# Group norm and gate of RWKV in four steps, laid beside the scan in another rhythm, and the first output columns ahead of the last units

## The chip, the cores and the metric

The kernel runs on one core of a Trainium2 chip. The metric is the device time of one execution in microseconds (us). The kernel before took 2945.2 us (median of three runs, 2944.56 to 2947.44).

## The reference, cut to what matters

One layer of an encoder over 1024 positions and 1024 channels, all in float32. Between two feed-forward halves stands a mixer. Its RWKV branch ends, for the sum y of a forward and a backward scan with 8 heads of 64 channels, in a group norm, a bonus and a gate, and both branches then go through projections:

```
y = moveaxis(ys[:, 0] + flip(ys[:, 1], axis=0), 0, 1)
y = (y - mean) * rsqrt(var + GN_EPS)  * ln_w + ln_b        # mean, var per head
y = y + sum over dirs of sum(r * k_dir * r_k, per head) * v
y = (y * (sigmoid(gd) @ g2)) @ w_o
merged = sigmoid(g_hy) * y_hy + sigmoid(g_rw) * y_rw
x = x + merged @ w_out
```

## The kernel before, in words

Every dense product is three matmuls (`mm3`): operands are split into a high part (ScalarE) and a remainder (VectorE or GpSimd), and hi\*lo, lo\*hi and hi\*hi are summed in PSUM. A dense group of 128 output channels and 512 positions with 512 inputs is twelve matmuls of 128x512 (4 times 3), with 1024 inputs 24.

The sequence is cut into 8 blocks of 128 positions. `Rwkv.run` walks through them in about ten steps a block (it yields after each): products with the inverted matrix, the next block's scores and its triangular inversion on VectorE (`eliminate`: `rw_lt`, fourteen pairs of small `rw_el`/`rw_x` operations, `rw_xt`; L955 to L980), two halves of the scan (`psS`, `psY`), and four steps that finish the inverse. The backward scan's results are stored in DRAM at the mirrored block, so blocks b and 7-b are complete together.

The first 64 steps of the scan run beside the gates' columns (`mixer_gates`). The last 25 run beside two other generators: `hyena_out` (16 dense groups, PSUM tile `pz`) and units of norm and gate (`RwkvPost.unit(b, u)`): one unit takes the block pair (b, 7-b) and half of the channels, 128x512 numbers. It loads y of both directions, k_dir of both, r, v and the gate's operands (ten DMAs), multiplies by a block of ones (`rp_ones`: head sums, L1466, L1468), squares, forms the inverse deviation (`head_rstd_steps`: `rp_head`, VectorE's `hr_` chain, `ident`), multiplies by the gate (`rp_gd`, `rp_g2`, L1491) and stores to `d_yo`. Each unit's tiles have one buffer in that phase. Five units (pairs 3, 3, 2, 2, 1) run there in 25 steps, one per step of the scan. The other three, (1,1), (0,0), (0,1), run in `mixer_out` in lockstep after the scan, and then come the 16 dense groups of `rw_out` (`mo_ps`), in two halves of positions: the first half needs only blocks 2 to 5, the second the others. Each group's result is merged with `sg` and `mh` (four DMAs of 128 KB per group, L1528) and split. Then the PSUM pool is closed, and 16 groups of 24 matmuls with `w_out` follow (`wo_ps`, another pool of three banks).

PE matmuls issued through `InOrder` keep the order in which they were written. All else is ordered by the framework's scheduler at build time, one fixed queue per engine; all DMAs stand on SyncE's queue (SP). `w_st` and `z_st` share two buffers.

Of the kernel before, what the change touches and what calls it, by code (L numbers as in the profile page):

```python
# [773 lines left out]
def head_rstd_steps(nc, te, ve, pool, rb, psum, sq, head, ident, scale, lo, eps):  # L774


    n = sq.shape[1] // P
    ps = psum.tile([P, 512], F32, name="psA", tag="psA")
    for t in range(n):
        te.matmul(ps[:, 2 * t : 2 * t + 2], sq[:, ts(t, P)], head, start=True, stop=True)  # L780
# [24 lines left out]
    return out
# [370 lines left out]
def mixer_in(tc, I, ident, wp, hl, scl, h2, h2ctx, dr):  # L1176
# [3 lines left out]
    with ExitStack() as ctx:  # L1180
# [69 lines left out]
        def rwkv_tile(j, width, u, o):  # L1250
# [152 lines left out]
def split_half(nc, wp, pool, src):  # L1403

    hi, lo = [pool.tile([P, 4, 512], F32R, name=n, tag=n) for n in ("s_hi", "s_lo")]
    for h in range(2):
        st = wp.tile([P, 2, 512], F32, name="z_st", tag="w_st")
        for j in range(2):
            x = src(2 * h + j)
            nc.sync.dma_start(st[:, j] if len(x.shape) == 2 else st[:, j].rearrange("p (b t) -> p b t", t=P), x)  # L1410
        split_from(nc, hi[:, 2 * h : 2 * h + 2], lo[:, 2 * h : 2 * h + 2], st, "act", "dve")
    return hi, lo
# [6 lines left out]
class RwkvPost:  # L1419
# [15 lines left out]
    def bank(self):  # L1435
        return self.psum.tile([P, 512], F32, name="psA", tag="psA")

    def unit(self, b, u):

        nc, te, dr, I = self.nc, self.te, self.dr, self.I  # L1440
        ve = nc.vector
        sl = slice(b, 8 - b, 7 - 2 * b)
        flat = lambda x: x.rearrange("p b q t -> p (b q t)")
        g = {}
        for n, m, d in (("y0", "y", 0), ("y1", "y", 1), ("k0", "kd", 0), ("k1", "kd", 1), ("r", "r", 0), ("v", "v", 0)):
            g[n] = self.work.tile([P, 2, 2, P], F32, name="rp_" + n)
            nc.sync.dma_start(g[n], dr[m][d][:, sl, 2 * u : 2 * u + 2])
        gd, g2 = [], []
        for n, r in ((0, slice(0, P)), (1, slice(P, P + 32))):
            rows = r.stop - r.start  # L1450
            gd.append(self.work.tile([P, 2, P], F32, name=f"rp_gd{n}")[0:rows])
            nc.sync.dma_start(gd[n], dr["gd"][r].rearrange("p (b t) -> p b t", t=P)[:, sl])
            g2.append(self.work.tile([P, 2, P], F32, name=f"rp_g2{n}")[0:rows])
            nc.sync.dma_start(g2[n], I["rw_g2"][r, ts(u, 256)].rearrange("p (q c) -> p q c", c=P))
        yield
# [18 lines left out]
        norm = head_rstd_steps(nc, te, ve, self.work, lambda: g["k1"].rearrange("p b q (e f) -> p (b q) e f", e=2), self.psum,
                               sq, self.head, self.ident, 1.0 / 64.0, None, GN_EPS)
# [7 lines left out]
        ve.tensor_tensor(flat(y), flat(y), pb, ALU.mult)  # L1483
# [3 lines left out]
        yield  # L1487
        ps = self.psum.tile([P, 2, 2, P], F32, name="psA", tag="psA")
        for q in range(2):
            for n in range(2):  # L1490
                te.matmul(ps[:, :, q], g2[n][:, q], gd[n], start=n == 0, stop=n == 1)  # L1491
# [5 lines left out]
def mixer_out(tc, I, ident, wp, dr, yp, early, begin, done, half_done):  # L1497
# [3 lines left out]
    with ExitStack() as ctx:  # L1501
        pool = lambda name, bufs, **k: ctx.enter_context(tc.tile_pool(name=name, bufs=bufs, **k))
        one = pool("mo1", 1)
        m_hi = one.tile([P, KD, L], F32R, name="m_hi")
        m_lo = one.tile([P, KD, L], F32R, name="m_lo")
        with ExitStack() as c2:
            pool2 = lambda name, bufs, **k: c2.enter_context(tc.tile_pool(name=name, bufs=bufs, **k))
            yb, two = pool2("mo2", 1), pool2("mo3", 2)
            pm, pq = pool2("mop", 3, space=PSUM), pool2("mopq", 4, space=PSUM)
            halves = lambda t: lambda q: dr["yo"][:, 4 * t : 4 * t + 4, q]  # L1510
# [6 lines left out]
            blocks = lambda a, j: a[ts(j, P)].rearrange("p (b t) -> p b t", t=P)  # L1517
            for t in range(2):
                if t:
                    y.append(split_half(nc, wp, yb, halves(1)))  # L1520
                for j in range(KD):
                    w = col_weights(nc, wp, I["rw_out"][:, ts(j, P)], 4, lo_eng="dve")
                    sg, mh = [two.tile([P, 512], F32, name=n) for n in ("mo_sg", "mo_mh")]
                    for x, n in ((sg, "sg"), (mh, "mh")):
                        x4 = x.rearrange("p (b t) -> p b t", t=P)
                        for h in range(2):
                            b = ORDER[4 * t + 2 * h]
                            nc.sync.dma_start(x4[:, ts(h, 2)], blocks(dr[n], j)[:, b : b + 2])  # L1528
# [23 lines left out]
def hybrid_layer_kernel(ctx: ExitStack, tc: tile.TileContext, I: dict, out: bass.AP):  # L1552
# [60 lines left out]
    with ExitStack() as c2:  # L1613
# [3 lines left out]
        with ExitStack() as c3:  # L1617
# [5 lines left out]
            def units():  # L1623
                todo = [post.unit(b, u) for b, u in ((3, 0), (3, 1), (2, 0), (2, 1), (1, 0))]
                next(todo[0])
                for g, n in zip(todo, todo[1:] + [None]):
                    for i in range(5):
                        if next(g, None) is None and i == 4 and n:
                            next(n)
                        yield  # L1630

            bg = units()
# [4 lines left out]
            for g in (bg, hy):  # L1637
                for _ in g:
                    pass
    with ExitStack() as ctx2:  # L1640
# [17 lines left out]
        mixer_out(tc, I, ident, wp, dr, zp, early, begin, lambda d, t: live["nm"].add(live["xT"][:, d, ts(t, 512)], t), normed)  # L1658
# [49 lines left out]
```

## Time and profile before

| | us |
|---|---|
| median of three runs | 2945.2 |
| the profiled execution | 2941.74 |
| its span | 2939.9 |
| PE busy | 2733.1 (93%) |
| DVE busy | 1233.9 (42%) |
| ACT busy | 905.4 (31%) |

PE is TensorE's matmuls, DVE VectorE, ACT ScalarE, POOL GpSimd, SP SyncE's DMA queue. Times of day ("at 1990") are us from the span's start. A square bracket in a timeline row is the engine's idle time before the row and what ended it.

### The profile page before, as it was taken

Reading aid. Unit: us, or ns where it says so; the run is one execution under the profiler, and the core shown is the slowest. Engines: PE = TensorE matmul, PEld = TensorE weight load, DVE = VectorE, ACT = ScalarE, POOL = GpSimd, SP = SyncE. Lnnn points to the kernel's source line nnn. Section 1 sums busy time; section 2 is a strip of 40 time slices with the busy share of each in tenths; the row PEclk is TensorE's granted clock in tenths of the full one; section 3 lists DMA queues with packets and bytes.
Section 4 is the critical chain, followed back from the end, with each engine's and each line's share of the span. In section 5 each row is a group of like instructions: output and inputs, shape, how many; then the busy total and the mean of one; then the engine's idle time right before and its main releaser. Section 6 shows DMA issues by size and latency. Waiting matters only on the chain. (4 is left out here: it accounts for less than half of the span.)

```text
span 2939.9 us, 46164 instructions
## 1 busy us (share of the span) xinstructions
PE 2733.1 (93%) x19440; PEld 2207.4 (75%) x19440; DVE 1233.9 (42%) x2142; ACT 905.4 (31%) x1515; POOL 549.9 (19%) x351
## 2 busy tenths in 40 slices
PE   7999999999788899996899998897899999999998
PEld 6888888888566677774777777675678888888887
DVE  4111010110556769798565567655560101111014
ACT  4111111111355543334454454421332111111112
POOL 2323233232422200000000000000023332323322
PEclk8999999999899999998999999897999999999999
DMA  4111111111432345545435335446731111111112
GB/s 122 51 43 54 40 58 43 40 57 44 154 82 76 111 148 170 166 125 161 114 101 157 101 104 153 150 126 199 224 101 43 51 53 40 58 43 52 46 29 90
DMA packets 414494, 277.66 MB, mean 94 GB/s; under 512 B 53571, under 2 KB 377359, under 8 KB 413648
## 3 DMA queue, kind: packets, MB, share of 16 engines
q1 hardware_dynamic: 414288, 274.72, 31.7%
q8 instruction: 153, 2.51, 0.4%
q14 instruction: 53, 0.43, 0.0%
HBM read 203.75 MB, written 70.91 MB: 93 GB/s over the span
## 5 line engine op out<-in xcount | busy, mean ns | idle before, releaser
L43 PE MATMUL pgu<-hThi,w_hi 128*128 128x512 f32 x1408 | 554.0, 393 | 0.9 <-issue 0.8
L45 PE MATMUL pgu<-hThi,w_lo 128*128 128x512 f32 x1408 | 551.4, 392 | 0.0
L44 PE MATMUL pgu<-hTlo,w_hi 128*128 128x512 f32 x1408 | 547.3, 389 | 0.5 <-DVE hTlo L37 0.3
L210 DVE TENSOR_TENSOR silu<-silu,pgu 128x512 f32<-128x512 f32 x88 | 60.5, 688 | 892.2 <-PE pgu L45 882.8
L33 ACT CAST w_hi<-w_st 128x1024 fp32r<-128x1024 f32 (+1 forms) x180 | 175.1, 974 | 531.2 <-PE pgu L44 320.4
L37 POOL TENSOR_TENSOR w_lo<-w_st,w_hi 128x1024 fp32r<-128x1024 f32 x100 | 240.4, 2404 | 419.2 <-ACT w_hi L33 419.1
L45 PEld LDWEIGHTS pgu<-hThi,w_lo 128*128 128x128 f32 x1408 | 264.3, 188 | 60.7
L44 PEld LDWEIGHTS pgu<-hTlo,w_hi 128*128 128x128 f32 x1408 | 264.3, 188 | 59.5 <-DVE hTlo L37 0.7
L43 PEld LDWEIGHTS pgu<-hThi,w_hi 128*128 128x128 f32 x1408 | 264.6, 188 | 55.0 <-issue 1.2
L43 PE MATMUL pdn<-g_hi,wd_hi 128*128 128x512 f32 x704 | 275.6, 391 | 3.1 <-DVE xT L227 3.1
L44 PE MATMUL pdn<-g_lo,wd_hi 128*128 128x512 f32 x704 | 275.1, 391 | 2.0 <-POOL g_lo L37 2.0
L45 PE MATMUL pdn<-g_hi,wd_lo 128*128 128x512 f32 x704 | 275.4, 391 | 1.5 <-POOL wd_lo L37 1.5
L227 DVE SCALAR_TENSOR_TENSOR xT<-pdn,xT 128x512 f32<-128x512 f32 x192 | 132.4, 690 | 315.3 <-PE pdn L45 315.3
L43 PE MATMUL pw<-hThi,w_hi 128*128 128x512 f32 (+1 forms) x448 | 185.2, 413 | 17.6 <-DVE nm_h L123 10.0
L45 PE MATMUL pw<-hThi,w_lo 128*128 128x512 f32 (+1 forms) x448 | 185.1, 415 | 12.1 <-DVE w_lo L1224 12.1
L37 POOL TENSOR_TENSOR wd_lo<-wdst,wd_hi 128x512 fp32r<-128x512 f32 (+1 forms) x112 | 133.0, 1189 | 332.7 <-ACT wd_hi L33 330.0
L37 POOL TENSOR_TENSOR g_lo<-silu,g_hi 128x512 fp32r<-128x512 f32 x88 | 113.9, 1294 | 397.2 <-ACT g_hi L33 397.2
L44 PE MATMUL pw<-hTlo,w_hi 128*128 128x512 f32 (+1 forms) x448 | 183.4, 409 | 0.0
L33 ACT CAST wd_hi<-wdst 128x512 fp32r<-128x512 f32 (+1 forms) x112 | 64.4, 576 | 378.7 <-PE pdn L44 361.6
L37 POOL TENSOR_TENSOR hTlo<-nm_h,hThi 128x512 fp32r<-128x512 f32 x16 | 23.1, 1445 | 841.7 <-ACT hThi L33 841.7
L43 PEld LDWEIGHTS pdn<-g_hi,wd_hi 128*128 128x128 f32 x704 | 132.5, 188 | 31.9 <-ACT wd_hi L33 4.2
L44 PEld LDWEIGHTS pdn<-g_lo,wd_hi 128*128 128x128 f32 x704 | 132.6, 188 | 30.7 <-POOL g_lo L37 2.9
(312 smaller groups left out, 4259.2 us busy)
## 6 DMA issues: line engine op xcount, KB each, us to landing
w_st<-in_ffn_w_gu SPq DMA_DIRECT2D x88, 512.0 KB, 3.8
w_st<-in_w_in SPq DMA_DIRECT2D x59, 512.0 KB, 4.3
wdst<-in_ffn_w_down SPq DMA_DIRECT2D x64, 256.0 KB, 2.8
wdst<-in_ffn_w_down SPq DMA_DIRECT2D x48, 192.0 KB, 2.4
d_kf<-kout SPq DMA_DIRECT2D x32, 256.0 KB, 3.6
hy_k<-d_kf SPq DMA_DIRECT2D x32, 256.0 KB, 3.2
w_st<-in_w_out SPq DMA_DIRECT2D x16, 512.0 KB, 5.3
d_X<-sh_x SPq DMA_DIRECT2D x12, 512.0 KB, 3.5
```

The lines of the kernel that those rows point to most:

```text
L33: nc.scalar.copy(hi, src)
L37: eng.tensor_tensor(lo, src, hi.bitcast(F32), ALU.subtract)
L43: te.matmul(out, lhs[0], rhs[0], start=first, stop=False)
L44: te.matmul(out, lhs[0], rhs[1], start=False, stop=False)
L45: te.matmul(out, lhs[1], rhs[0], start=False, stop=last)
L210: nc.vector.tensor_tensor(sl, sl, pu, ALU.mult)
L227: nc.vector.scalar_tensor_tensor(xa, ps, 0.5, xa, ALU.mult, ALU.add)
```

## The change

A unit has four steps instead of five: its loads are a function of their own (`load`, k and r ahead of y), the gate's product stands in the last step, the sum of both y behind the k operations. In the 25 scan steps a table decides: units skip the steps i % 10 = 3 and 4 (scores with inversion, first half of the scan), so 5 units and the first step of the sixth run there; dense groups of `hyena_out` fall on i % 10 = 0, 2, 3, 4, 6, 8, and on the first four of the last five. `mixer_out` takes up the sixth unit, loads both units of pair 0 in one set of ten DMAs twice as wide, and has the first weights, gates and the first half of `y` (`y0`) issued before. Gate and merge loads cover two groups each (256 KB DMAs), and `w_out`'s groups use the same four PSUM banks (`mo_ps`) as `rw_out`'s. The mixer's own projections compute the same numbers. The core of the diff:

```
+    def load(self, b, n):
...
+        for k, m, d in (("k0", "kd", 0), ("k1", "kd", 1), ("r", "r", 0), ("y0", "y", 0), ("y1", "y", 1), ("v", "v", 0)):
+            nc.sync.dma_start(g[k], dr[m][d][:, sl, 2 * u0 : 2 * u0 + n])
...
@@ unit @@
-        ve.tensor_tensor(flat(y), flat(y), flat(g["y1"]), ALU.add)
         for i in range(2):
             ve.tensor_tensor(k[:, i], k[:, i], g["k1"][:, 1 - i, :, ::-1], ALU.add)
         for q in range(2):
             ve.scalar_tensor_tensor(k[:, :, q], g["r"][:, :, q], vec(q, 2), k[:, :, q], ALU.mult, ALU.mult)
+        ve.tensor_tensor(flat(y), flat(y), flat(g["y1"]), ALU.add)
         yield
...
@@ mixer_out @@
-            pm, pq = pool2("mop", 3, space=PSUM), pool2("mopq", 4, space=PSUM)
-            y = [split_half(nc, wp, yp, halves(0))]
-            post = RwkvPost(nc, nc.tensor, I, dr, ident, pool2("mo4", 1), pool2("mo5", 3), pq)
-            units = [post.unit(b, u) for b, u in ((1, 1), (0, 0), (0, 1))]
-            for _ in range(6):
-                for g in units:
-                    next(g, None)
+            pq = pool2("mopq", 3, space=PSUM)
+            w = [weights(0), weights(1)]
...
+            gates(0, 0)
+            g = post.load(0, 4)
+            units = [rest, post.unit(0, 0, g(0)), post.unit(0, 1, g(1))]
+            while units:
+                units = [u for u in units if next(u, u) is not u]
...
-        pm = pool("mop2", 3, space=PSUM)
...
@@ beside the scan @@
             for i, _ in enumerate(rw):
-                next(bg, None)
-                if (i + 1) * 16 // 25 > i * 16 // 25:
-                    next(hy, None)
+                last = i >= 20
+                if last or i % 10 not in (3, 4):
+                    next(unit)
+                    at += 1
+                    if at % 4 == 0:
+                        b, u = todo[at // 4]
+                        unit = post.unit(b, u, post.load(b, (u, 2))(u))
+                if i % 10 in ((0, 1, 2, 3) if last else (0, 2, 3, 4, 6, 8)):
+                    next(hy)
...
+            y0 = split_half(nc, wp, zp, lambda st, h: nc.sync.dma_start(st, dr["yo"][:, 0:4, 2 * h : 2 * h + 2]))
```

On PE, behind the last matmuls of the dense groups `pz` and of the scan (`psY`), stood before the three units' sums (`rp_ones`) and squares (`rp_head`):

```order
L55 MATMUL pz<-s_hi,w_lo 128x512
L1466 MATMUL psA<-rp_y_17657,rp_ones 128x512
L1468 MATMUL psA<-rp_k_17661,rp_ones 128x512
L1466 MATMUL psA<-rp_y_17677,rp_ones 128x512
L1468 MATMUL psA<-rp_k_17681,rp_ones 128x512
L1466 MATMUL psA<-rp_y_17697,rp_ones 128x512
L1468 MATMUL psA<-rp_k_17701,rp_ones 128x512
L780 MATMUL psA<-rp_head,rp_y_17659 128x2 x4
```

and stands now:

```order
L55 MATMUL psY<-rw_t_16287,rw_s 64x64 x8
L55 MATMUL psA<-rp_y_17541,rp_ones 128x512
L55 MATMUL psA<-rp_k_17543,rp_ones 128x512
L43 MATMUL mo_ps<-s_hi,w_hi 128x512
L44 MATMUL mo_ps<-s_lo,w_hi 128x512
L45 MATMUL mo_ps<-s_hi,w_lo 128x512
L43 MATMUL mo_ps<-s_hi,w_hi 128x512
L55 MATMUL psA<-rp_head,rp_y_17542 128x2 x4
```

One unit's sums stand there, then the dense groups begin: 36 matmuls of `mo_ps` stand ahead of the sums of pair 0, 16 more ahead of its first `ident`, 5 ahead of the last, and 135 behind them.

On DVE, the end of the first inversion in this phase (`rw_x` last pair to `rw_xt`) had a unit's sum of y in it:

```order
L973 TENSOR_TENSOR rw_x<-rw_x,rw_el 128x14
L1458 TENSOR_TENSOR rp_y_15504<-rp_y_15504,rp_y_15506 128x512
L978 STREAM_TRANSPOSE rw_t<-rw_lt 128x16x2x16
L1090 TENSOR_TENSOR rw_s<-psS,rw_ptot 128x256
L980 STREAM_TRANSPOSE rw_xt<-rw_t 128x512
```

and now has the end of one unit and the start of the next behind it, ahead of the sum into `rw_t` that the inverse goes on with:

```order
L980 STREAM_TRANSPOSE rw_t<-rw_lt 128x16x2x16
L1092 TENSOR_TENSOR rw_s<-psS,rw_ptot 128x256
L982 STREAM_TRANSPOSE rw_xt<-rw_t 128x512
L1504 TENSOR_TENSOR rp_y_14905<-rp_y_14905,psA 128x512
L1506 TENSOR_SCALAR rp_y_14905<-rp_y_14905,rp_vec 128x2x128 x2
L1507 TENSOR_TENSOR rp_y_14905<-rp_y_14905,rp_k_14907 128x512
L1508 TENSOR_TENSOR rp_y_14905<-rp_y_14905,psA 128x512
L1476 TENSOR_TENSOR rp_k_15623<-rp_k_15623,rp_k_15624 128x256 x2
L1478 SCALAR_TENSOR_TENSOR rp_k_15623<-rp_r,rp_vec,rp_k_15623 128x2x128 x2
L1405 SCALAR_TENSOR_TENSOR z_sg<-z_sg,pz 128x512
L37 TENSOR_TENSOR w_lo<-w_st,w_hi 128x512
L1000 TENSOR_TENSOR rw_t<-rw_t,psA 128x16x16
```

The next unit's `rp_k` loads and, one row later, its `rp_y` loads wait for the tiles of the unit before (one buffer).

On SP, the scan's last stores (`d_y<-rw_y`) were followed by the constants of a second `RwkvPost` and the first of the thirty loads of the three units:

```order
L1099 DMA d_y_77<-rw_y 128x512
L1494 DMA d_yo<-rp_y_17110 128x2x256
L1426 DMA rp_head<-in_c_head 128x2
L1431 DMA rp_vec<-in_rw_ln_w 128x4x1
L1399 DMA d_mh<-z_sg 128x512
L1432 DMA rp_vec<-in_rw_ln_b 128x4x1
L1433 DMA rp_vec<-in_rw_r_k 128x4x1
L1447 DMA rp_y_17657<-d_y_76 128x2x256
L1447 DMA rp_y_17659<-d_y_77 128x2x256
```

and the queue now reads:

```order
L1453 DMA rp_y_17541<-d_y_76 128x2x256
L172 DMA w_st<-in_rw_out 128x4x128
L1101 DMA d_y_76<-rw_y 128x512
L1101 DMA d_y_77<-rw_y 128x512
L172 DMA w_st<-in_rw_out 128x4x128 x2
L1539 DMA mo_sg<-d_sg 128x512 x2
L1539 DMA mo_mh<-d_mh 128x512 x2
L1453 DMA rp_k_17689<-d_kd_78 128x2x512
L1453 DMA rp_k_17690<-d_kd_79 128x2x512
L1453 DMA rp_r<-d_r_68 128x2x512
L1453 DMA rp_y_17687<-d_y_76 128x2x512
L1453 DMA rp_y_17688<-d_y_77 128x2x512
```

The loads of pair 0 now stand behind three weight loads, of which the third waits for the first group's remainder `w_lo` (it frees the buffer), and behind the first merge loads.

## Rows read from the trace of the kernel before

**Rows 1.** The page: the span, and busy time by engine.

```profile
span 2939.9 us, 46164 instructions
PE 2733.1 (93%) x19440; PEld 2207.4 (75%) x19440; DVE 1233.9 (42%) x2142; ACT 905.4 (31%) x1515; POOL 549.9 (19%) x351
```

**Rows 2.** Windows: stretch, its length, busy us of each engine (instructions), granted TensorE clock, DMA busy share, GB/s. The scan beside the gates; three parts of the scan beside units and `pz`; the three units; `rw_out`; the gap; `w_out`.

```profile
1470.00:1790.00 320.00, 295.23 (x5743) 244.52 (x5742) 189.93 (x386) 159.81 (x344) 0.00 (x0) 0.97 0.39 112
1790.00:1835.00 45.00, 40.38 (x695) 33.29 (x697) 39.11 (x91) 19.49 (x43) 0.00 (x0) 0.95 0.66 202
1835.00:1860.00 25.00, 18.18 (x452) 14.38 (x448) 10.18 (x26) 11.49 (x23) 0.00 (x0) 0.85 0.56 162
1860.00:1990.00 130.00, 120.40 (x1944) 95.49 (x1943) 78.48 (x168) 45.78 (x98) 0.00 (x0) 0.87 0.43 134
1990.00:2035.00 45.00, 29.31 (x87) 16.95 (x87) 24.18 (x61) 6.15 (x11) 0.00 (x0) 0.66 0.61 188
2035.00:2087.00 52.00, 46.89 (x191) 36.81 (x189) 38.16 (x58) 18.89 (x29) 0.00 (x0) 0.93 0.76 229
2087.00:2096.00 9.00, 0.65 (x2) 0.50 (x2) 7.06 (x10) 2.18 (x3) 0.00 (x0) 0.76 0.81 216
2096.00:2187.00 91.00, 90.53 (x400) 74.16 (x398) 52.26 (x67) 31.49 (x42) 11.22 (x6) 0.99 0.48 141
```

**Rows 3.** Timeline of PE from the last `pz` to `w_out`: start, us, what.

```profile
1989.56 0.40 PE L55 MATMUL pz<-s_hi,w_lo 128*128 128x512 f32 x1
1998.45 2.05 PE L1466 MATMUL psA<-rp_y,rp_ones 128*128 128x512 f32 x2 [8.49 <-DVE rp_y L1458]
2015.95 5.12 PE L780 MATMUL psA<-rp_head,rp_y 128*128 128x2 f32 x24
...
2035.97 0.39 PE L43 MATMUL mo_ps<-s_hi,w_hi 128*128 128x512 f32 x1
2038.03 0.39 PE L43 MATMUL mo_ps<-s_hi,w_hi 128*128 128x512 f32 x1
...
2095.51 0.76 PE L43 MATMUL wo_ps<-m_hi,w_hi 128*128 128x512 f32 x1 [8.35 <-DVE mo_sg L1532]
```

**Rows 4.** Timeline of DVE in the first inversion: its start, the unit's waits in it, its end.

```profile
1821.19 1.12 DVE L962 STREAM_TRANSPOSE rw_lt<-rw_a 128x512 f32<-128x512 f32 x1
...
1827.47 0.42 DVE L1461 TENSOR_TENSOR rp_k<-rp_k,rp_k 128x256 f32<-128x256 f32 x1 [1.34 <-DMA rp_k<-d_kd]
...
1838.68 0.69 DVE L1458 TENSOR_TENSOR rp_y<-rp_y,rp_y 128x512 f32<-128x512 f32 x1 [2.57 <-DMA rp_y<-d_y]
...
1840.51 0.67 DVE L980 STREAM_TRANSPOSE rw_xt<-rw_t 128x512 f32<-128x512 f32 x1
```

**Rows 5.** Waits of PE from 1790 to 1990: who waited for whom, us in total, times, longest.

```profile
PE psA L55 <- DVE rw_xt L980: 7.0, 2, 4.9
...
PE psA L55 <- DVE rp_k L796: 3.0, 2, 1.7
```

**Rows 6.** Timeline of PE beside the end of the scan, one unit's matmuls and the last scan half.

```profile
1961.95 1.13 PE L55 MATMUL psA<-rp_y,rp_ones 128*128 128x512 f32 x2
1962.92 1.02 PE L55 MATMUL psA<-rp_k,rp_ones 128*128 128x512 f32 x2
...
1973.40 1.05 PE L55 MATMUL psA<-rp_head,rp_y 128*128 128x2 f32 x8
...
1978.41 1.16 PE L55 MATMUL psA<-ident,rp_k 128*128 128x128 f32 x8
...
1982.26 1.15 PE L55 MATMUL psY<-rw_SC,rw_AV 128*64 128x64 f32 x32
1983.35 1.15 PE L55 MATMUL psY<-rw_t,rw_s 64*64 64x64 f32 x32
1984.42 2.58 PE L55 MATMUL psA<-rp_gd,rp_g 128*128 128x256 f32 x8
```

**Rows 7.** Timeline of DVE: a unit's last multiply, and the next unit's sum of y, which needs the tile stored and loaded again.

```profile
1953.93 0.68 DVE L1492 TENSOR_TENSOR rp_y<-rp_y,psA 128x512 f32<-128x512 f32 x1
1961.21 0.69 DVE L1458 TENSOR_TENSOR rp_y<-rp_y,rp_y 128x512 f32<-128x512 f32 x1 [6.20 <-DMA rp_y<-d_y]
```

**Rows 8.** Timeline of SP: that store and that load.

```profile
1954.64 0.36 SPq L1494 DMA_DIRECT2D d_yo<-rp_y  x1
1957.36 1.31 SPq L1447 DMA_DIRECT2D rp_y<-d_y  x1
```

**Rows 9.** Windows (columns as in rows 2) while the units' loads run.

```profile
1996.00:2002.00 6.00, 3.29 (x4) 1.00 (x4) 2.94 (x6) 0.61 (x1) 0.00 (x0) 0.50 1.08 364
2002.00:2010.00 8.00, 4.03 (x5) 0.80 (x4) 4.35 (x9) 0.65 (x2) 0.00 (x0) 0.71 1.10 351
```

**Rows 10.** Timeline of DVE: the last merge of `rw_out`, and the first use of `xT`, which is loaded behind it.

```profile
2094.67 0.69 DVE L1532 SCALAR_TENSOR_TENSOR mo_sg<-mo_sg,mo_ps 128x512 f32<-128x512 f32 x1 [0.62 <-DMA mo_sg<-d_sg]
...
2111.36 1.29 DVE L1546 SCALAR_TENSOR_TENSOR xT<-wo_ps,xT 128x512 f32<-128x512 f32 x2 [6.62 <-DMA xT<-d_x]
```

**Rows 11.** Timeline of PE behind the second inversion: the first products with the inverse.

```profile
1926.17 1.26 PE L55 MATMUL psA<-rw_xt,rw_a 32*32 32x16 f32 x128 [2.15 <-DVE rw_xt L980]
1927.36 0.86 PE L58 MATMUL psA<-ident,rw_t 64*128 64x64 f32 x16
...
1931.55 1.26 PE L55 MATMUL psA<-rw_t,rw_z 32*32 32x16 f32 x128
```

More of the change, by code (lines that the diff above doesn't have):

```diff
@@ L774, in head_rstd_steps @@
 def head_rstd_steps(nc, te, ve, pool, rb, psum, sq, head, ident, scale, lo, eps):
-    n = sq.shape[1] // P
+    n = len(sq)
     ps = psum.tile([P, 512], F32, name="psA", tag="psA")
     for t in range(n):
-        te.matmul(ps[:, 2 * t : 2 * t + 2], sq[:, ts(t, P)], head, start=True, stop=True)
+        te.matmul(ps[:, 2 * t : 2 * t + 2], sq[t], head, start=True, stop=True)
     yield
@@ L795, in head_rstd_steps @@
     rb = rb()
-    ve.tensor_copy(rb, r.rearrange("p (t h) -> p t h", h=2).unsqueeze(3).to_broadcast([P, n, 2, 64]))
+    a, c = rb.shape[1:3]
+    ve.tensor_copy(rb, r.rearrange("p (a c) -> p a c", a=a).unsqueeze(3).to_broadcast([P, a, c, 64]))
     yield
@@ L801, in head_rstd_steps @@
         for q in range(4):
-            te.matmul(pb[:, ts(q, P)], rb[:, 4 * h + q].rearrange("p a b -> p (a b)"), ident,
+            i = 2 * (4 * h + q)
+            te.matmul(pb[:, ts(q, P)], rb[:, i // c, i % c : i % c + 2].rearrange("p a b -> p (a b)"), ident,
                       start=True, stop=True)
@@ L1263, in rwkv_tile @@
                     pb = yield from head_rstd_steps(
-                        nc, te, ve, t1, lambda: tmp.tile([P, 8, 2, 64], F32, name="hr_b", tag="sh_v"), pk, kh, head, ident, 4.0, 1e-24, 0.0)
+                        nc, te, ve, t1, lambda: tmp.tile([P, 1, 16, 64], F32, name="hr_b", tag="sh_v"), pk,
+                        [kh[:, ts(i, P)] for i in range(L // P)], head, ident, 4.0, 1e-24, 0.0)
                     yield
@@ L1389, in hyena_out, with rows @@
     for t in range(2):
-        z = split_half(nc, wp, zp, lambda q: dr["z"][ts(q, P)][:, ts(t, 512)])
+        def rows(st, h):
+            for q in range(2):
+                nc.sync.dma_start(st[:, :, q], dr["z"][ts(2 * h + q, P)][:, ts(t, 512)].rearrange("p (b t) -> p b t", t=P))
+        z = split_half(nc, wp, zp, rows)
         for j in range(8):
@@ L1405, in split_half @@
     hi, lo = [pool.tile([P, 4, 512], F32R, name=n, tag=n) for n in ("s_hi", "s_lo")]
+    view = lambda x, h: x[:, 2 * h : 2 * h + 2].rearrange("p q (b t) -> p b q t", t=P)
     for h in range(2):
[L1407 to L1411, printed above, removed]
+        st = wp.tile([P, 4, 2, P], F32, name="z_st", tag="w_st")
+        src(st, h)
+        split_from(nc, view(hi, h), view(lo, h), st, "act", "dve")
     return hi, lo
@@ L1433, in __init__, with part @@
         nc.sync.dma_start(v[:, :, 2], I["rw_r_k"].rearrange("h n -> (h n)").rearrange("(t p) -> p t", p=P))
[L1435 to L1440, printed above, removed]
-        ve = nc.vector
[L1442 to L1455, printed above, removed]
+    def load(self, b, n):
+        nc, dr = self.nc, self.dr
+        sl = slice(b, 8 - b, 7 - 2 * b)
+        u0, n = n if isinstance(n, tuple) else (0, n)
+        g = {}
+        for k, m, d in (("y0", "y", 0), ("y1", "y", 1), ("k0", "kd", 0), ("k1", "kd", 1), ("r", "r", 0), ("v", "v", 0)):
+            g[k] = self.work.tile([P, 2, n, P], F32, name="rp_" + k)
+        gd = [self.work.tile([P, 2, P], F32, name=f"rp_gd{i}")[0 : (P, 32)[i]] for i in range(2)]
+        g2 = [self.work.tile([P, n, P], F32, name=f"rp_g2{i}")[0 : (P, 32)[i]] for i in range(2)]
+        for k, m, d in (("k0", "kd", 0), ("k1", "kd", 1), ("r", "r", 0), ("y0", "y", 0), ("y1", "y", 1), ("v", "v", 0)):
+            nc.sync.dma_start(g[k], dr[m][d][:, sl, 2 * u0 : 2 * u0 + n])
+        for i, r in ((0, slice(0, P)), (1, slice(P, P + 32))):
+            nc.sync.dma_start(gd[i], dr["gd"][r].rearrange("p (b t) -> p b t", t=P)[:, sl])
+            nc.sync.dma_start(g2[i], self.I["rw_g2"][r, 256 * u0 : 256 * u0 + n * P].rearrange("p (q c) -> p q c", c=P))
+        def part(u):
+            q = slice(2 * (u - u0), 2 * (u - u0) + 2)
+            o = {k: x[:, :, q] for k, x in g.items()}
+            o["gd"], o["g2"] = gd, [x[:, q] for x in g2]
+            return o
+        return part
@@ L1456, in unit @@
+    def unit(self, b, u, g):
+        nc, te, dr = self.nc, self.te, self.dr
+        ve = nc.vector
+        flat = lambda x: x.rearrange("p b q t -> p b (q t)")
+        bank = lambda: self.psum.tile([P, 2, 2 * P], F32, name="psA", tag="psA")
         y, k = g["y0"], g["k0"]
         vec = lambda q, j: self.vec[:, 2 * u + q, j : j + 1]
-        ve.tensor_tensor(flat(y), flat(y), flat(g["y1"]), ALU.add)
         for i in range(2):
@@ L1482, in unit @@
             pb = end.value[0]
-        ve.tensor_tensor(flat(y), flat(y), pb, ALU.mult)
+        ps = self.psum.tile([P, 2, 2, P], F32, name="psA", tag="psA")
+        for q in range(2):
+            for n in range(2):
+                te.matmul(ps[:, :, q], g["g2"][n][:, q], g["gd"][n], start=n == 0, stop=n == 1)
+        ve.tensor_tensor(flat(y), flat(y), pb.rearrange("p (b x) -> p b x", b=2), ALU.mult)
         for q in range(2):
@@ L1486, in unit @@
         ve.tensor_tensor(flat(y), flat(y), flat(k), ALU.add)
[L1487 to L1491, printed above, removed]
         ve.tensor_tensor(flat(y), flat(y), flat(ps), ALU.mult)
@@ L1494, in unit, with mixer_out @@
         nc.sync.dma_start(dr["yo"][:, i0 : i1 + 1 : i1 - i0, 2 * u : 2 * u + 2], y)
-def mixer_out(tc, I, ident, wp, dr, yp, early, begin, done, half_done):
+        yield
+def mixer_out(tc, I, ident, wp, dr, post, rest, y0, early, begin, done, half_done):
     nc = tc.nc
@@ L1517, in mixer_out, with gates @@
-            blocks = lambda a, j: a[ts(j, P)].rearrange("p (b t) -> p b t", t=P)
+            pq = pool2("mopq", 3, space=PSUM)
+            weights = lambda j: col_weights(nc, wp, I["rw_out"][:, ts(j, P)], 4, lo_eng="dve")
+            w = [weights(0), weights(1)]
+            merge = {}
+            def gates(t, i):
+                out = []
+                for n in ("sg", "mh"):
+                    x = two.tile([P, 2, 512], F32, name="mo_" + n)
+                    for j in range(2):
+                        a = dr[n][ts(2 * i + j, P)].rearrange("p (h t) -> p h t", t=256)
+                        nc.sync.dma_start(x[:, j].rearrange("p (h t) -> p h t", t=256), a[:, 1:3] if t == 0 else a[:, 0::3])
+                    out.append(x)
+                merge[t, i] = out
@@ L1518, in mixer_out @@
+            gates(0, 0)
+            post.te, post.work, post.psum = nc.tensor, pool2("mo5", 1), pq
+            g = post.load(0, 4)
+            units = [rest, post.unit(0, 0, g(0)), post.unit(0, 1, g(1))]
+            while units:
+                units = [u for u in units if next(u, u) is not u]
+            y = [y0]
             for t in range(2):
                 if t:
-                    y.append(split_half(nc, wp, yb, halves(1)))
+                    y.append(split_half(nc, wp, yb, lambda st, h: nc.sync.dma_start(st, dr["yo"][:, 4:8, 2 * h : 2 * h + 2])))
@@ L1521, in mixer_out @@
                 for j in range(KD):
[L1522 to L1528, printed above, removed]
+                    if j % 2 == 0 and (t, j // 2) not in merge:
+                        gates(t, j // 2)
@@ L1529, in mixer_out @@
+                    sg, mh = [x[:, j % 2] for x in merge[t, j // 2]]
+                    wj = w.pop(0) if w else weights(j)
                     ps = pm.tile([P, 512], F32, name="mo_ps", tag="mo_ps")
                     for k in range(4):
-                        mm3(nc, ps, (w[0][:, k], w[1][:, k]), (y[t][0][:, k], y[t][1][:, k]), k == 0, k == 3)
+                        mm3(nc, ps, (wj[0][:, k], wj[1][:, k]), (y[t][0][:, k], y[t][1][:, k]), k == 0, k == 3)
                     nc.vector.scalar_tensor_tensor(sg, sg, 1.0, ps, ALU.add, ALU.mult)
@@ L1540, in mixer_out @@
                 w = col_weights(nc, wp, I["w_out"][:, ts(j, P)], KD, lo_eng="dve")
-                ps = pm.tile([P, 512], F32, name="wo_ps", tag="wo_ps")
+                ps = pm.tile([P, 512], F32, name="mo_ps", tag="mo_ps")
                 for k in range(KD):
@@ L1621, in hybrid_layer_kernel @@
             post = RwkvPost(nc, InOrder(tc), I, dr, ident, one, work, pq)
[L1623 to L1632, printed above, removed]
-            for i, _ in enumerate(rw):
-                next(bg, None)
-                if (i + 1) * 16 // 25 > i * 16 // 25:
-                    next(hy, None)
-            for g in (bg, hy):
-                for _ in g:
-                    pass
+            todo = [(3, 0), (3, 1), (2, 0), (2, 1), (1, 0), (1, 1)]
+            unit = post.unit(3, 0, post.load(3, (0, 2))(0))
+            at = 0
+            for i, _ in enumerate(rw):
+                last = i >= 20
[7 more added lines that the diff above has]
+                    next(hy)
+            for _ in hy:
+                pass
+            y0 = split_half(nc, wp, zp, lambda st, h: nc.sync.dma_start(st, dr["yo"][:, 0:4, 2 * h : 2 * h + 2]))
     with ExitStack() as ctx2:
@@ L1656, in normed @@
             live["nm"].apply(live["xT"], live["nm"].rows(t), t, live["hl"])
-        mixer_out(tc, I, ident, wp, dr, zp, early, begin, lambda d, t: live["nm"].add(live["xT"][:, d, ts(t, 512)], t), normed)
+        mixer_out(tc, I, ident, wp, dr, post, unit, y0, early, begin, lambda d, t: live["nm"].add(live["xT"][:, d, ts(t, 512)], t), normed)
         xT, np_ = live["xT"], live["np"]
```

15 lines of the change are left out of this document (8 added, 7 removed).

## The prediction

> **What bounds the kernel now.** The page first: TensorE is busy for 2733.1 of 2939.9 us, no other engine for half of that [rows 1], so a gain must come from stretches in which PE waits or runs at the lower of its two clock levels. The windows by stage find them [rows 2]: from 2096 on PE is all but full at 0.99, beside the gates too (0.97). Beside units and scan (1790 to 1990) the granted clock falls to 0.85 and 0.87, and from 1990 to 2096 PE is busy for 29.31 of 45, 46.89 of 52 and 0.65 of 9 us, the first of these at 0.66. The timeline of PE shows why [rows 3]: from the last `pz` matmul (1989.56 + 0.4) to the first of `w_out` (2095.51) pass 105.5 us, which begin with a wait of 8.49 for the first unit's sum, then the units alone, at low clock, then the dense groups, and end with a wait of 8.35 for a merge. The waits and the DVE timeline show the scan stretch [rows 4, 5].
>
> **The stretch behind the scan.** I call T0 the end of PE's last scan and `pz` matmul, 1990.0 before. What PE has to do between T0 and `w_out` at 2.4 GHz: 192 dense matmuls at 0.229 us apart (nine starts from 2035.97 to 2038.03 [rows 3]), 44.0; three units of 1.13 + 1.02 + 1.05 + 1.16 + 2.58 = 6.94 [rows 6], 20.8. That is 64.8 of 105.5; the other 40.7 are waits and low clock. The change adds no operation there; it moves dense matmuls between the units. What is late next, walked along PE's new order:
>
> - Unit (1,1) comes first. Its y tile is the one that unit (1,0) stores. A store, a load and the sum took from 1954.61 to 1961.21, 6.6 us [rows 7, 8]. Unit (1,0)'s multiply needs its gate product, and behind that PE has 12 `pz` matmuls (2.75) and a scan half (2.2 [rows 6]), so it ends at T0 - 4.3, and the sum starts at T0 + 2.3: PE waits until T0 + 3.0.
> - Two sums (2.2), 36 dense matmuls (8.2) and the squares (1.0) lead to T0 + 14.4.
> - The loads of pair 0: SP stands at the third `w_st` until `w_lo`, which DVE does right behind unit (1,1)'s sum, about T0 + 3.7. Up to both y loads 0.25 + 1.0 + 1.5 + 1.0 = 3.75 MB go out, at some 350 GB/s [rows 9] 10.7 us, and with some 3 us until the first has landed (the load of [rows 8] was issued at 1957.36 and used at 1961.21 [rows 7], less its own transfer) T0 + 17.4. With the two sums on DVE that is T0 + 18.5: PE waits 4.1.
> - Four sums (4.3), the first unit's spread and gate (3.7), squares (2.1), 16 dense (3.7): T0 + 32.3. The next spread needs eleven DVE operations behind the squares, some 5 us against 3.7 of dense work: 1.3 more. Spread and gate twice with 5 dense between (8.6): T0 + 42.2. 39 dense (8.9): T0 + 51.1.
> - The second half of y needs the last unit's multiply (T0 + 43), store and load (6.6) and the split (2.2): T0 + 51.8, a wait of 0.7. Both `z_st` hold the weights' buffers, so the second weight of that half is late by about 3. 96 dense matmuls (22.0): T0 + 76.8.
> - `w_out` follows without the 8.35: its groups share four banks with `mo_ps`, and m of the first half is long split. xT, loaded behind the last merge, was there 16 us after that merge [rows 10]; four groups of 24 matmuls are 22 us of cover.
> - Low clock behind the two long waits: before, the sums and squares there took 2.05 and 5.12 / 3 = 1.7 instead of 1.13 and 1.05 [rows 3, 6]. For eight sums and squares and some dense matmuls I add 4 (bounds 0 and 12; twelve would be all the unit work at half speed, as 0.66 [rows 2] comes near).
>
> Together some T0 + 81, against T0 + 105.5: a gain of 24.5. The transfers of the stretch also bound it: it moved 45 x 188 + 52 x 229 + 9 x 216 GB/s [rows 2] = 22.3 MB, of which a unit's 1.7 MB now comes earlier. 20.6 MB need 59 us at 350 GB/s and 90 at 229. I take the former's side, since ten DMAs per two groups become six and buffers reach two pairs ahead; 90 us is the other end, a gain of 16.
>
> The Trainium skill puts a DMA's fixed cost at about 2 us, most of it the write receipt, with HBM the slowest target (DMA: Bandwidth & Descriptors, Anatomy of one DMA). By that a store and a load of 256 KB would be 5.2 us by its formula, an estimate, and the first wait 1.4 shorter; the 6.6 of the trace, with SP's other entries between, is the better.
>
> **The stretch beside the scan.** The first inversion ran from 1821.19 to 1841.2 with two waits of 1.34 and 2.57 for a unit's loads in it [rows 4], besides unit operations of 0.4 to 0.7, and PE waited 4.9 at its end, 7.0 with the second [rows 5]. Without these DVE needs some 16 us, and PE has 18.0 to do in that time: two dense groups (5.5), two scan halves (8.8, twice the 2.2 of [rows 6], since the last one feeds no next state), spread and gate (3.7). The 7.0 shrink to about 0.5. But a wait comes in. The unit that ends now does so behind `rw_xt` (four operations of 0.7, as the multiply of [rows 7]: 2.8), then store, load and sum (7.3): its successor's sums, which PE must pass before the next product of the inverse, can start 10.1 after `rw_xt`, while PE's work up to there is 7.1 (1.26 + 0.86 + 2.75 + 1.26 + 0.86 [rows 11] with one dense group). That is 3 us, twice. And the first dense group now stands ahead of products that need no weights: up to 2. So the waits balance: +6.5 - 6 - 2, and one wait for `rp_k` of 1.7 less.
>
> What remains is the clock. With g = 0.85 and 0.87 PE spent 2 x (0.15 x 25 + 0.13 x 130) = 41 us at 1.2 GHz; if all of it were at 2.4, up to 20 us would come back; if the new waits fall worse, some 5 are lost. I take 5: a quarter, since the dense groups are still 16 in 25 steps, unlike the one per step of the gates' stretch with 0.97, but fall closer to the inversion. The first step of unit (1,1) in this stretch (its loads and sums on DVE) costs nothing: DVE is busy for 78.5 of the last 130.
>
> **Sum.** 24.5 + 5 = 29.5 off the profiled 2941.7 gives 2912; the median of the runs is 3.5 above that execution, so 2916.
>
> **The rivals.**
> 1. *Transfers bound the new stretch.* For it: DMA at 0.76 busy from 2035 to 2087 while PE waited. Against it: 350 GB/s elsewhere. At 229 GB/s the stretch takes 90 us, the gain is 16, with nothing from the scan: 2929.
> 2. *The clock stays low behind each wait*: the units' matmuls and the dense groups between them run at 1.2 GHz from T0 + 3 to T0 + 45, and the scan stretch gives nothing. For it: 0.66 in the units' stretch, also while PE had work. 12 instead of 4: a gain of 16.5, 2929. The skill says that waits on DMAs between short bursts of matmuls throttle the clock again each time (TensorE: Matmul & The Clock Gate, HAM oscillation); 0.66 agrees with it.
> 3. *The scan stretch gains its clock back*: 15 to 20 instead of 5. For it: inversion waits preceded the slow stretches. Against it: new waits. 24.5 + 16 gives 2905.
> 4. *The units' one buffer holds up the scan*: slower. Each of five unit changes lets PE stand for a store, a load and a sum (7.3), as PE's order in the scan is fixed and the next products queue behind the sums. If nothing covers it, 5 x 7.3 = 36.5 is lost against 24.5 + 6.5: 2951. It decides from (24.5 + 6.5) / 5 = 6.2 per change on. Against it: 7.1 us and more of other work stand between at every change.
> 5. *The groups don't come ahead*: the new order has 36 of them there. That leaves nothing for this.
>
> **Chances.** Forecast 0.56 (own range 2908 to 2924), rival 1 0.14, rival 2 0.13, rival 3 0.12, rival 4 0.05. The range from 2902 to 2934 takes in rivals 1 to 3 and leaves out 4 and the tails. A run can tell 0.2% (6 us) from no change. Faster 0.91 (the forecast and rivals 1 to 3 but for their tails), same 0.04, slower 0.05.
>
> **What would show it.** In the profile after: the time from the last scan matmul to the first `w_out` matmul, some 81 (right between 73 and 90); the wait before `w_out` gone; one wait of some 3 before unit (1,1)'s sums and one of some 4 before those of pair 0; PE's wait for `rw_xt` under 2, and new waits at the unit's sums behind it; the granted clock of the last 200 us of the scan above 0.87. A span of that scan stretch longer than before by over 5, or dense groups waiting for `w_st` and `mo_sg` for over 10 in all, would make the forecast wrong.

## The result, and the profile after

The changed kernel took 2928.2 us (median of four runs) against 2944.9 (four runs): ratio 0.9943, 95% interval 0.9926 to 0.9960. It is faster by 16.7 us; 29 were forecast. Measured a second time it took 2926.5 (five runs) against 2946.1 (eight), ratio 0.9936 (0.9909 to 0.9963). Two executions of the experiments below, of 4150 and 5021 us, ran at a far lower clock and are left out of every time given here. The page answers to [rows 1]:

```profile
span 2927.1 us, 46056 instructions
PE 2726.0 (93%) x19440; PEld 2201.1 (75%) x19440; DVE 1235.5 (42%) x2141; ACT 907.8 (31%) x1517; POOL 549.9 (19%) x351
```

PE lost 7.1 us of busy time and 5.7 of idle time. The span tells more when it is cut at four places that both kernels have: the last matmul of the gates' columns, T0 (the end of the last scan and `pz` matmul), the first `w_out` matmul, and the first of the second feed-forward half. First come the windows between them of before, then of after (columns as in [rows 2]):

```profile
1782.80:1990.00 207.20, 182.45 (x3168) 145.88 (x3166) 134.89 (x294) 83.15 (x175) 0.00 (x0) 0.88 0.50 150
1990.00:2095.50 105.50, 76.35 (x276) 53.78 (x277) 68.89 (x128) 27.22 (x43) 0.00 (x0) 0.80 0.70 211
2095.50:2187.40 91.90, 91.06 (x401) 74.71 (x401) 53.02 (x67) 31.89 (x43) 11.22 (x6) 0.98 0.49 142
```

```profile
1785.60:1989.70 204.10, 180.92 (x3168) 144.36 (x3166) 138.21 (x298) 87.23 (x176) 0.00 (x0) 0.89 0.52 159
1989.70:2077.40 87.70, 70.44 (x278) 51.05 (x276) 62.63 (x120) 24.28 (x41) 0.00 (x0) 0.88 0.73 228
2077.40:2173.70 96.30, 92.23 (x400) 74.54 (x401) 56.87 (x71) 33.40 (x44) 11.21 (x6) 0.98 0.49 142
```

| stretch | before | after | difference | forecast |
|---|---|---|---|---|
| up to the scan stretch | 1782.8 | 1785.6 | +2.8 | 0 |
| scan beside units and `pz` | 207.2 | 204.1 | -3.1 | -5 |
| T0 to `w_out` | 105.5 | 87.7 | -17.8 | -24.5 |
| `w_out` | 91.9 | 96.3 | +4.4 | 0 |
| the rest | 752.5 | 753.4 | +0.9 | 0 |

The first line is chance: PE's order there is the same in both kernels, and in three profiles of the kernel before that line reads 1782.8, 1793.6 and 1791.7. What PE waited for between T0 and `w_out` (us in total, times, longest), and the timeline of PE at these places, which answers to [rows 3]:

```profile
PE mo_ps L43 <- ACT w_hi L33: 5.9, 1, 5.9
PE psA L1482 <- DVE rp_y L1479: 5.2, 1, 5.2
PE psA L55 <- DVE rp_y L1479: 4.0, 1, 4.0
PE psA L804 <- issue: 1.1, 1, 1.1
```

```profile
1993.71 1.10 PE L55 MATMUL psA<-rp_y,rp_ones 128*128 128x512 f32 x2 [3.99 <-DVE rp_y L1479]
...
2011.61 2.08 PE L1482 MATMUL psA<-rp_y,rp_ones 128*128 128x512 f32 x2 [5.17 <-DVE rp_y L1479]
...
2051.73 0.80 PE L43 MATMUL mo_ps<-s_hi,w_hi 128*128 128x512 f32 x1 [5.89 <-ACT w_hi L33]
2052.32 0.63 PE L44 MATMUL mo_ps<-s_lo,w_hi 128*128 128x512 f32 x1
...
2077.42 0.50 PE L43 MATMUL mo_ps<-m_hi,w_hi 128*128 128x512 f32 x1 [1.10 <-ACT w_hi L33]
...
2102.46 0.50 PE L43 MATMUL mo_ps<-m_hi,w_hi 128*128 128x512 f32 x1 [1.90 <-ACT w_hi L33]
```

The wait of 8.35 ahead of `w_out` is now 1.1. Three waits stand where three were expected, each longer. After each, matmuls take longer for a while (2.08 in the row of 2011.61, 0.63 instead of 0.39 in the row of 2052.32), and the granted clock is lower, here in the window behind the first:

```profile
1994.00:1998.00 4.00, 4.00 (x10) 2.17 (x8) 1.98 (x3) 1.76 (x3) 0.00 (x0) 0.60 0.64 191
```

The wait of 1.90 in the last row stands inside `w_out`, where the kernel before had none.

### The profile page after: what moved, and what is told of

Read it like the earlier page. It is cut to its first block, busy times and chain, and to the rows that moved or that the text cites. A ratio compares the mean times of both kernels' runs of the same rounds, so it can differ in the third digit from the quotient of the medians.

```text
span 2927.1 us, 46056 instructions
## 1 busy us (share of the span) xinstructions
PE 2726.0 (93%) x19440; PEld 2201.1 (75%) x19440; DVE 1235.5 (42%) x2141; ACT 907.8 (31%) x1517; POOL 549.9 (19%) x351
```

## The experiments

Theory A says that each remaining wait has a cause of its own in the order of loads. Its rivals are that the transfers bound the stretch (B), that the order of groups does little (C), and others named with the runs. Every edit is against the changed kernel, and stretches are from each run's profile. An edit can move more than its own text, since the build-time scheduler orders all engines anew: ahead of pair 0's sums PE has 36 dense matmuls in the changed kernel, 24 with the own buffers below, and 12 in the last run.

**Half of xT later.**

```
-            for h in range(4):
-                nc.sync.dma_start(xT[:, :, ts(h, 256)], x_dram[:, :, ts(ORDER[2 * h] // 2, 256)])
+            def load(hs):
+                for h in hs:
+                    nc.sync.dma_start(xT[:, :, ts(h, 256)], x_dram[:, :, ts(ORDER[2 * h] // 2, 256)])
+
+            load((0, 1))
...
+                if (t, j) == (0, 2):
+                    nc.vector.tensor_copy(xT[:, 0, 512:769:256], xT[:, j, 0:2])
+                    load((2, 3))
```

> Edit against the changed kernel: only the first half of xT (2 MB) is loaded ahead of w_out; the second half is held back until the third group of w_out is done, so that the weights of groups 5 to 8 stand ahead of it. Theory A (w_out is 4.4 us longer than before because 4 MB of xT now stand behind four weights and no longer behind five, and the fifth weight is late): from the first w_out matmul to the first of the second feed-forward half 92 us instead of 96.3, no wait for w_hi near 25 us into it, the time some 4 us under the changed kernel (2924). Rival B (the longer w_out is only a lower clock behind the short waits at its start, one execution's chance): 96 again, no change (2928).

It took 2918.3 us (median of five runs), ratio 0.9911 (0.9892 to 0.9929). `w_out` takes 91.7, with no wait inside it over 0.85: theory A holds for `w_out`. The time fell by more than these 4.6 us; the profiled run's scan stretch, which the edit does not touch, was 7.0 shorter (197.1). SP in the changed kernel, then here:

```profile
2078.65 3.68 SPq L172 DMA_DIRECT2D w_st<-in_w_out  x2
2082.52 7.88 SPq L1679 DMA_DIRECT2D xT<-d_x  x4
2090.51 15.30 SPq L172 DMA_DIRECT2D w_st<-in_w_out  x4
```

```profile
2073.31 3.73 SPq L172 DMA_DIRECT2D w_st<-in_w_out  x2
2077.23 1.77 SPq L1683 DMA_DIRECT2D xT<-d_x  x2
2079.46 15.83 SPq L172 DMA_DIRECT2D w_st<-in_w_out  x4
2095.35 2.22 SPq L1683 DMA_DIRECT2D xT<-d_x  x2
```

The weights that follow xT go out 7.4 us after `w_out` began (2072.1) instead of 13.1. In the kernel before a fifth weight stood ahead of xT. The other profiles agree: with five weights ahead of the whole of xT, `w_out` takes 91.0 to 93.1 us (four profiles); with four, 94.8 to 97.6 (seven).

**Own buffers for the weights of `rw_out`.**

```
-    st = pool.tile([P, KD, P], F32, name="w_st", tag="w_st", bufs=2)[:, 0:kt, 0:width]
+    st = stage.tile([P, 4, P], F32, name="w_own") if stage else pool.tile([P, KD, P], F32, name="w_st", tag="w_st", bufs=2)[:, 0:kt, 0:width]
...
+            wo = pool2("mo6", 4)
```

> Edit against the changed kernel: the weights of rw_out get four staging buffers of their own instead of the two that they share with z_st. Theory A (single waits with a cause each): SP no longer stands 3.5 us at the third weight, so PE's wait for pair 0 falls from 5.2 to about 2; the wait of 5.9 for the weight of the second half falls to the 2 by which y itself is late, and the slow matmuls behind it (2 us) go. From the last scan matmul to the first of w_out 79 instead of 87.7; the time 2917 to 2921. Rival B (transfers bound the stretch): the waits move to the merge loads, at most 3 us are gained, 2925 to 2929.

It took 2915.8 us (median of five runs), ratio 0.9906 (0.9887 to 0.9926). Its profile is that of a second run:

> The kernel of the own weight buffers once more, for an undisturbed profile. Theory A: from the last scan matmul to the first of w_out 77 to 80 us, with PE's wait for pair 0 near 2, that for the second half's weight under 3; w_out near 92, since five weights now stand ahead of xT. Rival B (transfers bound the stretch): waits of together 10 us or more remain there, for merges or weights, and the stretch takes 85 or more.

The second run took 2921.6 (three runs), T0 to `w_out` 83.3, `w_out` 91.0. PE's waits:

```profile
PE psA L1482 <- DVE rp_y L1479: 5.8, 1, 5.8
PE psA L55 <- DVE rp_y L1479: 4.0, 1, 4.0
...
PE mo_ps L43 <- ACT w_hi L33: 1.1, 1, 1.1
```

This is half right. The wait of 5.9 for the second half's weight is gone (the 1.1 stands at the first group), and five weights stand ahead of xT again. The wait for pair 0 is as long as ever, but this does not clear SP's stand at the third weight as its cause, for the edit only moved the stand. SP, then DVE, in this profile:

```profile
1992.66 0.86 SPq L1101 DMA_DIRECT2D d_y<-rw_y  x2
1996.69 0.94 SPq L172 DMA_DIRECT2D w_own<-in_rw_out  x2
```

```profile
2007.82 0.69 DVE L1562 SCALAR_TENSOR_TENSOR mo_sg<-mo_sg,mo_ps 128x512 f32<-128x512 f32 x1 [3.88 <-PE mo_ps L45]
...
2011.20 1.42 DVE L1476 TENSOR_TENSOR rp_k<-rp_k,rp_k 128x256 f32<-128x256 f32 x4
...
2015.33 1.29 DVE L1479 TENSOR_TENSOR rp_y<-rp_y,rp_y 128x512 f32<-128x512 f32 x2
```

SP stands for 3.2 us ahead of the first weight with an own buffer (3.0 of it, by SP's waits, until the store of `d_y` has landed), about as long as at the third weight in the changed kernel. And pair 0's sum of y (row of 2015.33) starts here without idle time before it, some rows behind a merge for which DVE waited 3.88 on PE: what came last is DVE's other work, and no longer the load.

**Pair 0's loads first.** The line `g = post.load(0, 4)` moves ahead of `weights(1)` and `gates(0, 0)`.

> Edit against the changed kernel: pair 0's ten loads stand ahead of the first 1 MB of merge loads. Theory A: y of pair 0 is there 2.9 us sooner (1 MB at 350 GB/s), the wait of 5.2 falls to about 2.3, and 3 to 4 us are gained, since the merges have four PSUM banks behind them: 2924 to 2925. Rival B (transfers bound the stretch): the merges come later by as much, the groups wait for banks, no change (2928).

```profile
PE psA L1482 <- DVE rp_y L1479: 0.3, 1, 0.3
```

T0 to `w_out` takes 82.9 and the wait is gone, as theory A has it, although SP still stands at a weight for as long:

```profile
1995.93 3.60 SPq L172 DMA_DIRECT2D w_st<-in_rw_out  x2
```

The time, 2929.1 (0.9941, 0.9921 to 0.9962), does not show these 4.8 us: in the profiled run the stretch up to the scan was 2.7 us longer than in the changed kernel, the scan stretch 1.1 (205.2) and `w_out` 1.3 (97.6).

**Units beside the inversion.** The condition `i % 10 not in (3, 4)` becomes `i % 10 not in (8, 9)`; two profiles were taken.

> Edit against the changed kernel: beside the scan the units skip steps 8 and 9 of ten instead of 3 and 4, so that unit operations and their loads stand in VectorE's inversion again and PE's sums right behind the scan halves. Theory A (the inversion's waits are what the table removes, and new waits at the sums give half of it back): PE waits for rw_xt 5 to 9 us in all, the scan stretch from 1793.7 to 1989.7 gets 4 to 8 us longer: 2932 to 2936. Rival B (the table's place does not matter, the stretch is paid in the clock): within 2 us of the changed kernel, 2926 to 2930.

> The units beside the inversion once more: the first profile had 209.6 us in the scan stretch. Theory A (the table's place is worth 5 us or more): 206 to 211 again. Rival E: 199 to 204.

The times are 2931.4 (0.9952, 0.9934 to 0.9970) and 2929.7 (one run), the scan stretches 209.6 and 204.5. PE waits for `rw_xt` again, 4.0 us in both profiles and less than the 5 to 9 expected (in the changed kernel's list there is no such wait):

```profile
PE psA L55 <- DVE rw_xt L982: 4.0, 2, 2.5
```

**The scan stretch of both kernels again.**

> The kernel before once more, for a second profile of its scan stretch (from the last matmul of the gates' columns to the last of the scan: 207.2 us in the first profile; 197.1 to 205.2, mean 201.2, in seven profiles whose units and groups stand as in the changed kernel). Theory A (the new table is worth about 5 us there): 205 to 209. Rival E (the 207.2 was a chance of one execution, the table is worth nothing): 199 to 204.

> The kernel before a third time, as above. Theory A: 205 to 209. Rival E: 199 to 204.

> The changed kernel once more, beside the kernel before on this chip. Scan stretch 198 to 205, from the last scan matmul to w_out 86 to 90, w_out 95 to 98; the time 2924 to 2930.

The kernel before had 207.2, 207.0 and 207.6. Eight profiles with the changed table, in which PE's order there is the same, had 204.1, 201.4, 197.1, 201.6, 205.2, 201.4, 199.1 and 199.8, mean 201.2. The change is worth 6 us there and not the 3.1 of one pair of profiles. Whether that comes from keeping units out of the inversion stays open: with the units back beside it, 209.6 is longer than all eight, but 204.5 is not and misses its expectation. PE's idle time there was 22.5 and 23.4 us, within the 21.4 to 25.3 of the eight: the `rw_xt` waits came back, but not more waiting in sum.

In the next two stretches the changed kernel had 87.5 and 96.7 this time; the kernel before had 105.5 and 109.4 from T0 to `w_out`, against 105.5 in its first profile.

**All units ahead of the groups.** PE's matmuls of units and groups keep the written order (`InOrder`).

> Edit against the changed kernel: PE keeps the written order in this stage, so that all three units stand ahead of the first dense group; loads, banks and the scan's table stay as changed. Theory A (groups between the units are what fills PE's waits): the stretch from the last scan matmul to w_out goes from 87.7 to about 98, of which the 13.4 us of dense work that now stand between the units come behind them and only 3 are hidden otherwise: 2936 to 2941. Rival C (the loads issued earlier and the wider transfers do it, the order of the groups little): under 92 us, 2927 to 2932.

It took 2935.7 (0.9965, 0.9945 to 0.9985), and T0 to `w_out` 100.0: theory A. The wait that the groups had filled:

```profile
2010.03 2.05 PE L55 MATMUL psA<-rp_y,rp_ones 128*128 128x512 f32 x2 [12.62 <-DVE rp_y L1479]
```

**Another PSUM pool for `w_out`.**

```
-        pm = pool("mop", 4, space=PSUM)
+            pm = pool2("mop", 4, space=PSUM)
...
+        pm = pool("mop2", 3, space=PSUM)
```

> Edit against the changed kernel: the PSUM banks of rw_out are given back and w_out's groups use another pool of three, as before the change. Theory A (the wait of 8.35 ahead of w_out was that pool change): a wait of 5 to 8 us for the last merge returns ahead of the first w_out matmul, the stretch takes 93 to 96, and as w_out starts later its late weight costs less (w_out 92 to 94): 2930 to 2933. Rival D (the wait would be gone anyway, by the wider merge loads): no wait over 2 us there, 2928.

It took 2925.8 (0.9926, 0.9903 to 0.9948), and T0 to `w_out` 90.6:

```profile
2073.65 0.47 PE L43 MATMUL mo_ps<-m_hi,w_hi 128*128 128x512 f32 x1 [2.46 <-DVE mo_sg L1561]
```

This lies between the two: a wait for the last merge returns, but of 2.5 and not 5 to 8. It stands in the place of the 1.1 of the changed kernel. The whole time cannot tell 3 us.

**The three edits together** (half of xT later, own buffers, pair 0 first):

> The edits of half the xT loads, own weight buffers and pair 0's loads first, together. Theory A: the stretch from the last scan matmul to w_out in 74 to 78 us, w_out in 92, the time 2909 to 2915, below each of the single edits. Rival B (transfers bound it): the stretch stays above 80, the time 2915 to 2920, no better than the own buffers alone.

It took 2907.3 us, ratio 0.9862 (0.9839 to 0.9886), the fastest of all; T0 to `w_out` 77.5, `w_out` 91.5. Its window from T0 to `w_out`, to be read against the second one of after:

```profile
1984.30:2061.80 77.50, 69.90 (x278) 51.18 (x278) 59.46 (x116) 23.74 (x41) 0.00 (x0) 0.89 0.83 255
```

The same work and nearly the same bytes (77.5 us at 255 GB/s, 87.7 at 228) go through in 10 us less: rival B falls.

## Why the prediction was right or wrong

Direction, range and places were right: 2928.2 lies in 2902 to 2934, though outside the forecast's own 2908 to 2924. The gain was forecast too large: in the profiled pair it is 12.9 instead of 29.5. By the table, 6.7 are missing behind T0, 4.4 in `w_out`, 1.9 in the scan, and 3.7 (2.8 + 0.9) are stretches that the change leaves alone. The signs that were named came too: 87.7 lies between 73 and 90, PE no longer waits for `rw_xt`, and the granted clock of the scan stretch is 0.89.

- **T0 to `w_out` (81 forecast, 87.7).** The work is 64.8 in both sums; what is lost beside it was forecast at 16.1 and measured at 22.9, and no single step carries the difference:

| lost between T0 and `w_out` | forecast | after |
|---|---|---|
| wait for unit (1,1)'s sum | 3.0 | 4.0 |
| wait for pair 0's sums | 4.1 | 5.2 |
| wait for the last spread | 1.3 | 1.1 |
| wait at the second half (y and weight) | 3.7 | 5.9 |
| wait for the first weight of `w_out` | 0 | 1.1 |
| low clock (the rest) | 4 | 5.6 |

- **The first unit.** From the multiply's end to the sum passed 7.6 (1985.31 to 1992.92, rows below), where [rows 7] gave 6.6. By the formula of the Trainium skill (DMA: Bandwidth & Descriptors, Anatomy of one DMA) the estimate was 5.2. That lies further off; the formula is fitted there to DMAs issued from GpSimd, and all of these stand on SyncE's queue.
- **Pair 0.** Both sides were late: PE came at T0 + 16.7 and not 14.4, and y (DVE's row of 2010.87) at T0 + 21.2 and not 17.4. Of these 3.8, 2.3 were there when DVE had done the `w_lo` that frees the third weight's buffer (row of 1995.06): at T0 + 6.0 and not 3.7.
- **The second half.** The wait is not new: the kernel before had one of 5.1 at the same place (row below), more than the 3.7 forecast.

```profile
2061.82 0.80 PE L43 MATMUL mo_ps<-s_hi,w_hi 128*128 128x512 f32 x1 [5.08 <-ACT w_hi L33]
```

DVE in the changed kernel, then SP's store and load between its first two rows, and its stand at the third weight:

```profile
1984.62 0.69 DVE L1508 TENSOR_TENSOR rp_y<-rp_y,psA 128x512 f32<-128x512 f32 x1
...
1992.92 0.69 DVE L1479 TENSOR_TENSOR rp_y<-rp_y,rp_y 128x512 f32<-128x512 f32 x1 [0.29 <-DMA rp_y<-d_y]
1995.06 0.69 DVE L37 TENSOR_TENSOR w_lo<-w_st,w_hi 128x512 fp32r<-128x512 f32 x1 [1.46 <-ACT w_hi L33]
...
2010.87 1.29 DVE L1479 TENSOR_TENSOR rp_y<-rp_y,rp_y 128x512 f32<-128x512 f32 x2 [0.93 <-DMA rp_y<-d_y]
```

```profile
1985.44 0.41 SPq L1510 DMA_DIRECT2D d_yo<-rp_y  x1
...
1989.48 0.76 SPq L1453 DMA_DIRECT2D rp_y<-d_y  x1
...
1992.65 3.52 SPq L172 DMA_DIRECT2D w_st<-in_rw_out  x2
```

The load was issued 4.0 us after the store, more than in [rows 8] (2.7).

- **The cause named for pair 0** (SP held at the third weight) is neither shown nor ruled out. With the loads ahead of the merge loads the wait goes while the stand stays, so the stand alone does not make the wait; no run took the stand away. The cause named for the second half (`z_st` in the weights' buffers) fits: with own buffers that wait is gone.
- **The 8.35.** It went, but "its groups share four banks" explains little of it: with a pool of their own the wait is 2.5 instead of 1.1, and the stretch some 3 longer (90.6 against 87.7). What took away the other 6 was not tried by itself (the merge loads are wider and begin earlier).
- **Where the gain came from.** Of the 17.8, the order of groups between the units gives 12.3 (100.0 less 87.7) and the banks up to 3; the remaining 2.5 were not taken apart. These are single profiles with one thing undone in each, and need not add up; five profiles with the changed kernel's order of PE there lie between 86.5 and 88.7.
- **`w_out` at no cost: the step that failed.** It looked at xT's cover on the PSUM side (22 us, and that was enough: PE never waited for xT) and not at what stands behind xT on SP: the weights. Four weights ahead of 4 MB instead of five cost 4.4, and 1.9 of that is seen as one wait, the rest as short waits and low clock.
- **The scan stretch** came out near the forecast (6 for 5, on average; single executions of one order differ there by up to 8). The `rw_xt` waits of 7.0 went, and waits at the sums came (3.6 in four, not 6 in two). Over three profiles before and eight after, PE's busy time for the same 3168 matmuls fell from 181.7 to 178.3 us on average and its idle time from 25.6 to 23.0: a little more than half is clock, where the forecast had the waits balance and all of the 5 as clock. (The 7.1 of PE's work beside the new waits adds up to 7.0, which changes nothing.)
- **The rivals.** Rivals 1 and 2 gave 2929, the very time, by mechanisms that were not at work: 87.7 was no limit of the transfers (77.5 in the last run), and the low clock cost 5.6 and not 12. By the time alone they did better than the forecast; only the stretches tell them apart. The clock does fall anew behind each of the three long waits, by the window of 1994 and the rows of 2011.61 and 2052.32 above. The Trainium skill says that waits on DMAs between short bursts of matmuls throttle the clock anew each time (TensorE: Matmul & The Clock Gate, HAM oscillation); this trace agrees. The price was nearer the forecast's 4 than the rival's 12. Rival 3 (15 to 20 back in the scan) and rival 4 (a loss there) did not come.

## What to carry to other kernels

When work is moved so that a queue gets to a large load earlier, look at what stands behind that load in the queue, not only at who waits for the load itself. A wait that names its last semaphore has several candidates upstream: undo each alone before one is blamed or cleared, and look in the new trace whether it is really gone, for a stand can move to another place in the queue. And take several profiles and compare by stretches between landmarks: whole times here differ by 20 us between equal runs, single stretches by 1 to 11.

## What the runs showed of the hardware

The stretch ahead of the change's place, with PE's order unchanged, ended between 1782.8 and 1793.6 us in thirteen profiles. The scan stretch took 197.1 to 205.2 in eight executions of one order of PE: for 3168 equal matmuls PE was busy for 174.5 us where the granted clock was 0.93, and for 182.6 where it was 0.88. These differences by chance are as large as the smaller terms of the sum.
